# Block sums of weights for fourteen seven-product pairs: added in DRAM by transfers instead of on VectorE

## The chip, the cores and the metric

The kernel runs on one core of one Trainium2 chip. The metric is the device time of one execution in microseconds (us); the kernel before takes 1660.25 us, the median of 3 runs (1660.11 to 1660.39). Engines are named as in the profile: PE is TensorE's matmuls, PEld its weight loads, DVE is VectorE, ACT ScalarE, POOL GpSimd and SP SyncE. SP and Pool issue transfers here and compute nothing.

## The reference, cut to what matters

One block of a transformer on 256 positions of width 2048 in float32, with 256 positions of context beside it: a modulation of the inputs made from a condition vector, a gated recurrence in two directions with 8 heads, windowed attention with 8 heads, a gated merge of the two, and a feed-forward part with 5632 inner columns.

```python
mod = silu(cond) @ w_ada + b_ada                      # 6 vectors of 2048
px = modulate(x, norm1_g, mod[0], mod[1]) @ w_in       # the same for ctx
rec_x = recurrence(px...); att_x = windowed_attention(px...)
mix_x = gated_merge(rec_x, att_x, px[8], px[9], w_rec_proj, w_att_proj, w_out)
x_mid = x + mod[2] * mix_x
a, u = split(modulate(x_mid, norm2_g, mod[3], mod[4]) @ w_up)
ffn_x = (silu(depthwise_conv(a) ) * u) @ w_down
out = x_mid + mod[5] * ffn_x
```

The last four vectors of `mod` are needed late. The change concerns the product with `w_down` and, by where its transfers stand, the making of these vectors.

## The kernel before

All weights of the products lie in DRAM in one stream, `wst`, cut into halves of 128 x 1024 numbers (512 KB) in the order of their use. For each half SP issues a load into `raw` (five buffers), ACT rounds it to `whi`, DVE subtracts for the rest `wlo` (three buffers each), and PE multiplies with both: three matmuls stand for one product of full precision (`mm3`, L75). `Stream.load` (from L113) does this for most stages; `chunk` (from L144) for those where four blocks of 512 columns are combined.

The kernel runs the stages one after the other: the first projections, the modulation's first two vectors among them; the recurrence's gates and heads (`hgrn_a` to `hgrn_e`, tile `hb`); the attention (`att_scores`, `att_trans`, `att_out`); the gates and merge; `w_out`; the up products; the joint down stage (`down_two`); the last up and down products. Small work of the recurrence and the attention is kept in a list and put between the matmuls of the next products (`tick`).

The modulation's last four vectors are made beside all this. `ada_steps` (L476) is a generator of 128 steps. Each step loads a block of 512 KB into one of three or four `araw` buffers, by Pool's queue (L492), and DVE multiplies it by one column of the condition and adds it to `acc` (L495 for the first of 16 steps, L497 for the others). After 16 steps PE turns `acc` in two halves into PSUM (L505, pool `ms`, three banks, the same pool that the recurrence and the attention use) and DVE sums them into `modv`. `ada(n)` (L517) takes n steps at low priority; the stages call it at fixed places, and `Stream.load` by a pace.

In what order an engine gets its instructions is decided when the program is built: a scheduler places them by priority, by what they depend on and by its own notion of how long things take. On the chip each engine then works strictly in that order.

The joint down stage multiplies 16 pairs of blocks for each of two output halves. In seven of the 16 pairs (`SEVEN`) `half` (L175) uses seven products where eight would be needed; for that it wants, beside the blocks w21, w22 (load `rb`) and w11, w12 (load `ra`), four sums: t1 = w11 + w12, t3 = w12 + w22, t2 = t1 + w22, t4 = t2 + w21. DVE makes them by four additions of 128 x 512 (`four`, L228 to L231) into two `araw` buffers, and `chunk` rounds and splits these like loaded halves. The same function serves the gates' product (3 pairs in each of two halves) and the last down product.

Of the kernel before, what the change touches and what calls it, by code (L numbers as in the profile page):

```python
# [1 line left out]

# [5 lines left out]
F32 = mybir.dt.float32  # L8
# [3 lines left out]
ALU = mybir.AluOpType  # L12
AX = mybir.AxisListType

P = 128
T = 256
D = 2048
KT = D // P
# [16 lines left out]
FF_GROUPS = [(0, 16), (16, 16), (32, 12)]  # L35
SEVEN = (1, 3, 5, 7, 9, 11, 13)
# [18 lines left out]
def block_kernel(ctx, tc, xct, xr, prm, cst, ada2, wst, out):  # L55
    nc = tc.nc
# [9 lines left out]
    dram = ctx.enter_context(tc.tile_pool(name="dram", bufs=1, space=bass.MemoryType.DRAM))  # L66

    def bank(pool=None):
        pool = pool or mm
        return pool.tile([P, 512], F32, name="bank" + ("m" if pool is mm else "s"))  # L70
# [4 lines left out]
    def mm3(o, lh, ll, rh, rl, start, stop):  # L75
        mmul(o, lh, rh, start, False)
        mmul(o, lh, rl, False, False)
        return mmul(o, ll, rh, False, stop)
# [27 lines left out]
    class Stream:  # L106
# [26 lines left out]
        def next(self, n=1):  # L133
            if self.pos == 8:
                self.load()
            sl = slice(self.pos * P, (self.pos + n) * P)
            self.pos += n
            return self.hi[:, sl], self.lo[:, sl]

    st = Stream()  # L140
# [3 lines left out]
    def chunk(parts, make, tag="raw", home=None):  # L144
        with tc.high_priority(offset=min(LEAD, max(0, tc.tile_snap_priority() - base[0]))), ExitStack() as inorder:
            raw = strm.tile([P, 1024], F32, name=tag, bufs=5 if tag == "raw" else 2) if isinstance(tag, str) else tag
            hi, lo = home or [strm.tile([P, 1024], F32R, name=nm, bufs=3) for nm in ("whi", "wlo")]
            for b in behind:
                inorder.enter_context(tc.issue_after(b.ins))
            make(raw)  # L150
            w = slice(0, 512 * parts)
            a = S.copy(hi[:, w], raw[:, w])  # L152
            b = V.tensor_tensor(lo[:, w], raw[:, w], hi[:, w].bitcast(F32), op=ALU.subtract)  # L153
            behind[:] = [a, b]
        return raw, [(hi[:, 512 * i:512 * i + 512], lo[:, 512 * i:512 * i + 512]) for i in range(parts)]

    def fetch(raw):
        nc.sync.dma_start(raw, wst[st.half])
        st.half += 1

    def split(hi, lo, src):
        S.copy(hi, src)
        V.tensor_tensor(lo, src, hi.bitcast(F32), op=ALU.subtract)

    def combine(sev, y, post):
        S.copy(y[0], sev[0])
        V.tensor_tensor(y[2], sev[2], y[0], op=ALU.subtract)
        V.tensor_tensor(y[1], sev[1], y[2], op=ALU.add)
        V.tensor_tensor(y[2], sev[3], y[2], op=ALU.add)
        V.tensor_tensor(y[3], sev[3], y[1], op=ALU.add)  # L170
        if post:
            for b in range(4):
                post(b)

    def half(act, order, seven, sums, banks, y, own, made={}, post=None, tail=False):  # L175

        norm, sev = banks

        def add(b, a, w, start=False, stop=False):
            mm3(b, *a, *w, start, stop)  # L180
        seven = [p for p in order if p in seven]
        plains = [p for p in order if p not in seven]
        for p in order:
            k1, k2 = 2 * p, 2 * p + 1
            rb, (w21, w22) = chunk(2, fetch)
            a11, a21, a12, a22 = act(k1, 0), act(k1, 1), act(k2, 0), act(k2, 1)
            st0, plain = p == order[0], p == plains[0]
            if p not in seven:
                if p == order[-1]:
                    ra, (w11, w12) = chunk(2, fetch)  # L190
                    for b, u1, u2, v1, v2 in ((0, a11, a12, w11, w21), (1, a11, a12, w12, w22), (2, a21, a22, w11, w21),
                                              (3, a21, a22, w12, w22)):
                        for w in [slice(0, 512)] if not tail or b < 3 else [slice(0, 256), slice(256, 512)]:
                            add(norm[b][:, w], u1, [v[:, w] for v in v1])
                            add(norm[b][:, w], u2, [v[:, w] for v in v2], stop=True)
                    break
                add(norm[0], a12, w21, st0)
                add(norm[2], a22, w21, st0)
                add(norm[1], a12, w22, st0)
                add(norm[3], a22, w22, plain)  # L200
                ra, (w11, w12) = chunk(2, fetch)
                add(norm[0], a11, w11)
                add(norm[2], a21, w11)
                add(norm[1], a11, w12)
                add(norm[3], a21, w12)
                continue
            f, l = p == seven[0], p == seven[-1]
            if f:
                sev = sev()
            s1, s2, s4, *s3 = sums[p]  # L210
            add(norm[0], a12, w21, st0)
            add(norm[1], s4, w22, st0)
            ra, (w11,) = chunk(1, fetch, home=own)
            add(sev[0], a11, w11, f, l)
            if p in made:
                t1, t3, t2, t4 = made[p]
                add(sev[1], s1, t1, f, l)
                add(sev[3], s3[0] if s3 else a21, t3, f, l)
                add(sev[2], s2, t2, f, l)
                add(norm[2], a22, t4, st0)  # L220
                if l:
                    combine(sev, y, post)
                continue

            r4 = strm.tile([P, 1024], F32, name="araw", bufs=2)

            def four(raw):
                V.tensor_tensor(raw[:, 0:512], ra[:, 0:512], ra[:, 512:], op=ALU.add)  # L228
                V.tensor_tensor(raw[:, 512:], ra[:, 512:], rb[:, 512:], op=ALU.add)  # L229
                V.tensor_tensor(r4[:, 0:512], raw[:, 0:512], rb[:, 512:], op=ALU.add)  # L230
                V.tensor_tensor(r4[:, 512:], r4[:, 0:512], rb[:, 0:512], op=ALU.add)  # L231
            r2, (t1, t3) = chunk(2, four, "araw")
            add(sev[1], s1, t1, f, l)
            add(sev[3], s3[0] if s3 else a21, t3, f, l)

            _, (t2, t4) = chunk(2, lambda raw: None, r4)
            add(sev[2], s2, t2, f, l)
            add(norm[2], a22, t4, st0)
            if l:
                combine(sev, y, post)  # L240
        if post:
            return
        with tc.high_priority(offset=RUSH):
            for b in range(4):
                V.tensor_tensor(y[b], norm[b], y[b], op=ALU.subtract if b == 2 else ALU.add)
# [271 lines left out]
    def ada(n=1):  # L517
        with tc.high_priority(offset=-LAG), tc.issue_after(st.last.ins):
            for _ in range(n):
                next(ada_it, None)  # L520

    tasks = []

# [46 lines left out]
    def q_heads(h0):  # L570
        for h in range(h0, h0 + 4, 2):
            for i, o in enumerate(duo((xx, xx))):
                fold(qo[:, 0, h + i, :], o)
            ada(2)
        for h in range(h0, h0 + 4, 2):
            tmp = scr.tile([P, 512], F32, name="t")
            q2 = qo[:, 0, h:h + 2, :].rearrange("p h t -> p (h t)")
            exp_silu(q2, q2, tmp)
# [386 lines left out]
    for c in range(4):  # L965
        st.pace = 0
        if c % 2 == 0:
            norm = [bank() for _ in range(4)]
            y = [scr.tile([P, 512], F32, name="t") for _ in range(3)] + [scr.tile([P, 512], F32, name="rs", bufs=1)]
# [245 lines left out]
    def make(p, home):  # L1215
        rb, ra = [strm.tile([P, 1024], F32, name="raw", bufs=5) for _ in range(2)]
        for i, r in enumerate((rb, ra)):
            nc.sync.dma_start(r, wst[wst.shape[0] - 12 + 2 * LAST_ORDER.index(p) + i])
        r2, r4 = [strm.tile([P, 1024], F32, name="araw", bufs=2) for _ in range(2)]
        V.tensor_tensor(r2[:, 0:512], ra[:, 0:512], ra[:, 512:], op=ALU.add)  # L1220
        V.tensor_tensor(r2[:, 512:], ra[:, 512:], rb[:, 512:], op=ALU.add)
        V.tensor_tensor(r4[:, 0:512], r2[:, 0:512], rb[:, 512:], op=ALU.add)
        V.tensor_tensor(r4[:, 512:], r4[:, 0:512], rb[:, 0:512], op=ALU.add)
        for i, r in enumerate((r2, r4)):
            split(home[:, i, 0], home[:, i, 1], r)
        made[p] = [(home[:, i, 0, c:c + 512], home[:, i, 1, c:c + 512]) for i in range(2) for c in (0, 512)]
# [158 lines left out]
```

## Time and profile before

| what | us |
|---|---|
| median of 3 runs | 1660.25 |
| the profiled execution | 1660.26 |
| its span, first to last instruction | 1658.5 |
| PE busy | 1639.9 |
| DVE busy | 1303.1 |
| ACT busy | 861.8 |
| Pool busy | 68.7 |
| joint down stage, about | 1290 to 1457 |

The span is what the views of the profile divide up; 1.8 us of the execution lie around it. In the views, a group of instructions is a line, an engine, an operation and tiles, written out<-in with the count; then its busy time, the mean of one in ns, and the idle time before them with what ended it. A window is written as from:to, length, and then the busy time of PE, PEld, DVE, ACT and Pool, each with the number of instructions, the granted clock, the share of the DMA engines and GB/s. A wait is written as who, for whom, us in total, times and the longest.

### The profile page before, as it was taken

What the parts mean: (1) busy time and instruction counts of PE and PEld (TensorE: products, weight loads), DVE (VectorE), ACT (ScalarE), POOL (GpSimd) and SP (SyncE); (2) the same over time, 40 slices, a digit from 0 to 9 for tenths busy, and PEclk for the clock granted to TensorE, in tenths of its full rate; (3) what the DMA queues carried; (4) which work ended last, traced back from release to release, by engine and by line L of the source; (5) the groups of instructions that cost most, each with busy time, mean ns of one, the idle gap of its engine ahead of it and who ended that gap; (6) DMA issues with size and microseconds to landing.
All of it is one profiled execution on the core that took longest, in us unless ns stands there. A gap on an engine that the chain in (4) does not pass through costs nothing.

```text
span 1658.5 us, 23677 instructions
## 1 busy us (share of the span) xinstructions
PE 1639.9 (99%) x8827; PEld 1356.1 (82%) x8827; DVE 1303.1 (79%) x2001; ACT 861.8 (52%) x1302; POOL 68.7 (4%) x133
## 2 busy tenths in 40 slices
PE   7999999999999999999999999999999999999998
PEld 3668888888888888888888988888888888888887
DVE  3448986676889976888787798878877898998788
ACT  4336553443645664545445665555555555556552
POOL 0000100000000000000011000000000000000000
PEclk9999999999999999999999999999999999999999
DMA  9996834534455665676878467767655665666654
GB/s 380 408 373 241 300 115 153 204 114 150 167 205 202 222 215 176 233 284 213 310 262 307 175 238 263 251 226 267 235 193 185 203 207 199 222 207 222 220 186 162
DMA packets 104260, 377.03 MB, mean 227 GB/s; under 512 B 11696, under 2 KB 12112, under 8 KB 103888
## 3 DMA queue, kind: packets, MB, share of 16 engines
q1 hardware_dynamic: 85568, 307.87, 52.1%
q0 software_dynamic: 18576, 67.64, 12.4%
q8 instruction: 69, 1.13, 0.3%
q14 instruction: 47, 0.39, 0.1%
HBM read 373.36 MB, written 2.11 MB: 226 GB/s over the span
## 4 chain that ended last, share of the span: by engine, by line
PE 88%; DVE 4%; DMA 4%; issue 3%; ACT 1%; SPq 0%; POOL 0%; DVEq 0%; ACTq 0%; POOLq 0%
PE bankm L73 77%; PE banks L73 9%; DMA ringv<-in_wst_dram 1%; DMA ringq<-in_wst_dram 1%; DVE wlo L119 1%; DVE acc L497 1%; DMA ringkT<-in_wst_dram 1%; PE banks L505 0%; PE banks L872 0%; DMA araw<-in_ada_dram 0%; DMA xraw<-in_xct_dram 0%; ACT whi L118 0%; PE banks L697 0%; PE banks L705 0%; PE banks L900 0%
## 5 line engine op out<-in xcount | busy, mean ns | idle before, releaser
L73 PE MATMUL bankm<-hl,whi 128*128 128x512 f32 (+1 forms) x2048 | 626.6, 388 | 0.1
L118 ACT CAST whi<-raw 128x1024 fp32r<-128x1024 f32 (+1 forms) x378 | 394.5, 1045 | 393.2 <-PE bankm L73 338.9
L119 DVE TENSOR_TENSOR wlo<-raw,whi 128x1024 fp32r<-128x1024 f32 (+1 forms) x378 | 458.9, 1215 | 176.7 <-ACT whi L118 175.6
L73 PE MATMUL bankm<-whi,hl 128*128 128x512 f32 x1538 | 496.1, 393 | 1.3 <-ACT hl L340 0.9
L73 PE MATMUL bankm<-hl,wlo 128*128 128x256 f32 (+2 forms) x1760 | 396.1, 293 | 1.3 <-DVE wlo L119 1.3
L73 PEld LDWEIGHTS bankm<-hl,wlo 128*128 128x128 f32 x1760 | 330.5, 188 | 75.8 <-DVE wlo L119 2.1
L73 PEld LDWEIGHTS bankm<-hl,whi 128*128 128x128 f32 x2048 | 327.5, 189 | 17.7 <-DVE fs L1066 0.4
L73 PEld LDWEIGHTS bankm<-whi,hl 128*128 128x128 f32 x1538 | 288.0, 188 | 63.8 <-ACT hl L340 2.6
L73 PE MATMUL bankm<-wlo,hl 128*128 128x512 f32 x769 | 300.1, 391 | 0.0
L73 PEld LDWEIGHTS bankm<-wlo,hl 128*128 128x128 f32 x769 | 144.4, 188 | 28.9 <-DVE wlo L119 0.2
L497 DVE SCALAR_TENSOR_TENSOR acc<-araw,csil,acc 128x1024 f32<-128x1024 f32 x120 | 153.2, 1277 | 0.5
L153 DVE TENSOR_TENSOR wlo<-raw,whi 128x1024 fp32r<-128x1024 f32 x95 | 115.7, 1223 | 31.6 <-ACT whi L152 28.1
L152 ACT CAST whi<-raw 128x1024 fp32r<-128x1024 f32 x95 | 99.8, 1054 | 71.1 <-PE bankm L73 45.8
L492 POOL DMA_DIRECT2D araw<-in_ada_dram x128 | 67.9, 531 | 1111.9 <-DVE acc L497 635.5
L73 PE MATMUL bankm<-whi,yb 128*128 128x512 f32 x256 | 82.1, 396 | 0.0
L152 ACT CAST whi<-araw 128x1024 fp32r<-128x1024 f32 x44 | 46.2, 1053 | 62.4 <-DVE araw L229 56.2
L73 PEld LDWEIGHTS bankm<-whi,yb 128*128 128x128 f32 x256 | 47.9, 188 | 10.0
L153 DVE TENSOR_TENSOR wlo<-araw,whi 128x1024 fp32r<-128x1024 f32 x44 | 53.6, 1221 | 1.8 <-ACT whi L152 0.5
L73 PE MATMUL bankm<-wlo,yb 128*128 128x512 f32 x128 | 50.4, 394 | 0.0
L1079 ACT ACTIVATE fs<-fs,prm 128x256 f32<-128x256 f32 x44 | 26.4, 600 | 45.7 <-DVE fs L554 45.7
L73 PE MATMUL bankm<-whi,g 128*128 128x512 f32 x124 | 41.3, 389 | 0.0
L321 DVE TENSOR_REDUCE tn<-banks 128x8 f32<-128x32 f32 (+1 forms) x9 | 1.7, 187 | 46.1 <-ACT whi L118 42.9
(344 smaller groups left out, 1708.0 us busy)
## 6 DMA issues: line engine op xcount, KB each, us to landing
raw<-in_wst_dram SPq DMA_DIRECT2D x495, 512.0 KB, 4.0
araw<-in_ada_dram POOLq DMA_DIRECT2D x128, 512.0 KB, 4.6
ringv<-in_wst_dram SPq DMA_DIRECT2D x24, 512.0 KB, 9.9
ringq<-in_wst_dram SPq DMA_DIRECT2D x20, 512.0 KB, 9.9
araw<-in_wst_dram SPq DMA_DIRECT2D x10, 512.0 KB, 9.9
xraw<-in_xct_dram SPq DMA_DIRECT2D x8, 512.0 KB, 8.0
raw<-in_wst_dram SPq DMA_DIRECT2D x7, 384.0 KB, 9.9
ringkT<-in_wst_dram SPq DMA_DIRECT2D x5, 512.0 KB, 9.9
```

What stands on the lines that cost most here:

```text
L73: return PE.matmul(o, l, r, start=start, stop=stop, skip_group_check=True)
L118: S.copy(hi, raw)
L119: self.last = V.tensor_tensor(lo, raw, hi.bitcast(F32), op=ALU.subtract)
L152: a = S.copy(hi[:, w], raw[:, w])
L153: b = V.tensor_tensor(lo[:, w], raw[:, w], hi[:, w].bitcast(F32), op=ALU.subtract)
L321: V.tensor_reduce(m8, aps[:, 0:w].rearrange("p (q g c) -> p q c g", q=2 * n, g=4)[:, :, 0:2, :], axis=AX.X, op=ALU.add)
L492: nc.gpsimd.dma_start(raw, ada2[idx])
L497: V.scalar_tensor_tensor(acc, raw, csil[:, kt, 0:1], acc, op0=ALU.mult, op1=ALU.add)
L1079: S.activation(t, s, AF.Identity, bias=cb[:, f:f + 1], scale=cw[:, f, 1:2])
```

## The change

The fourteen seven-product pairs of the joint down stage (seven in each output half) get their four sums from DRAM. For each pair a block `sum` of 2 x 128 x 1024 numbers (1 MB) is laid out in DRAM. A copy fills it with `rb` and `ra` (L177 of the changed kernel), two transfers that add make t1 and t3 in its second part from `wst` (L179, L180), one makes t2 in the first part from t1 (L182) and one t4 from t2 (L184). All are issued by Pool's queue, four pairs at a time, one transfer per call of `ada`: 14 copies of 1 MB and 56 adding transfers of 256 KB, 70 in all. In the joint stage `half` then loads of `ra` only w11 (256 KB), and the two parts of the sum (512 KB each) by SP into the two `araw` buffers in which DVE built them before. DVE's four additions go; rounding, splitting and the matmuls stay. The other seven-product pairs are unchanged.

```diff
+    def fetch_half(raw):
+        nc.sync.dma_start(raw[:, 0:512], wst[st.half, :, 0:512])
+        st.half += 1
...
+    def sum_steps(group):
+        ds = []
+        for n, p in group:
+            at = JOINT + 32 * n
+            d = dram.tile([2, P, 1024], F32, name="sum%d" % len(dsums))
+            dsums[at, p] = d
+            ds.append((d, at + 2 * p))
+        for d, r in ds:
+            yield lambda: nc.gpsimd.dma_start(d, wst[r:r + 2])
+        for d, r in ds:
+            yield lambda: nc.gpsimd.dma_start(d[1, :, 0:512], wst[r + 1, :, 512:], accum_op=ALU.add)
+            yield lambda: nc.gpsimd.dma_start(d[1, :, 512:], wst[r, :, 512:], accum_op=ALU.add)
+        for d, r in ds:
+            yield lambda: nc.gpsimd.dma_start(d[0, :, 512:], d[1, :, 0:512], accum_op=ALU.add)
+        for d, r in ds:
+            yield lambda: nc.gpsimd.dma_start(d[0, :, 0:512], d[0, :, 512:], accum_op=ALU.add)
+
+    sum_all = [(n, p) for n in range(2) for p in SEVEN]
+    sum_it = (f for i in range(0, len(sum_all), 4) for f in sum_steps(sum_all[i:i + 4]))
...
-            ra, (w11,) = chunk(1, fetch, home=own)
+            ra, (w11,) = chunk(1, fetch_half if (at, p) in dsums else fetch, home=own)
...
+            if (at, p) in dsums:
+                d = dsums[at, p]
+                _, (t1, t3) = chunk(2, lambda raw: nc.sync.dma_start(raw, d[1]), "araw")
...
+                _, (t4, t2) = chunk(2, lambda raw: nc.sync.dma_start(raw, d[0]), "araw")
...
         with tc.high_priority(offset=-LAG), tc.issue_after(st.last.ins):
             for _ in range(n):
                 next(ada_it, None)
+            for f in itertools.islice(sum_it, 1):
+                f()
```

The change also moves instructions that it does not name, since the whole order is built anew. Lines of the changed kernel stand 1 to 43 higher than those of before (L497 is L538, L505 is L546, L119 is L120). Three places show it.

Pool's queue, from the start of the program. Before, it holds the modulation's loads one behind the other (`gate` is a late row of the first of the four vectors):

```order
L1380 UNCONDITIONAL_BRANCH
L492 DMA araw<-in_ada_dram 128x1024 x83
L955 DMA gate_7178<-line 128x1024
L492 DMA araw<-in_ada_dram 128x1024 x45
L1380 UNCONDITIONAL_BRANCH
```

After, with `sum_1149` and the next names for the blocks in DRAM:

```order
L1423 UNCONDITIONAL_BRANCH
L177 DMA sum_1149<-in_wst_dram 16x16384
L533 DMA araw<-in_ada_dram 128x1024 x4
L177 DMA sum_1150<-in_wst_dram 16x16384
L533 DMA araw<-in_ada_dram 128x1024
L177 DMA sum_1151<-in_wst_dram 16x16384
L533 DMA araw<-in_ada_dram 128x1024
L177 DMA sum_1152<-in_wst_dram 16x16384
L533 DMA araw<-in_ada_dram 128x1024
L179 DMA sum_1149<-in_wst_dram 128x512
```

The first copy has moved to the head of the queue, where one modulation load stood, and the other transfers stand between the loads.

DVE's order in the recurrence. Before, around half 35 of the weights (halves are counted here by their `wlo`), the modulation's steps stand singly or a few together between halves and the recurrence's instructions (`hb`, `qo`):

```order
L645 TENSOR_TENSOR hb<-hb,qo 128x256
L497 SCALAR_TENSOR_TENSOR acc<-araw,csil,acc 128x1024
L119 TENSOR_TENSOR wlo<-raw,whi 128x1024
L649 TENSOR_TENSOR hb<-hb 128x512
L497 SCALAR_TENSOR_TENSOR acc<-araw,csil,acc 128x1024
L554 TENSOR_TENSOR qo<-bankm,qo 128x256 x2
L119 TENSOR_TENSOR wlo<-raw,whi 128x1024
L497 SCALAR_TENSOR_TENSOR acc<-araw,csil,acc 128x1024
L254 TENSOR_TENSOR qo<-qo,t 128x512
L497 SCALAR_TENSOR_TENSOR acc<-araw,csil,acc 128x1024
L119 TENSOR_TENSOR wlo<-raw,whi 128x1024
```

After, the 16 halves up to half 61 stand together, and behind them come the steps that belong before and after half 35 in the order above:

```order
L670 TENSOR_SCALAR hb<-hb,lb_t 128x512
L120 TENSOR_TENSOR wlo<-raw,whi 128x1024 x16
L538 SCALAR_TENSOR_TENSOR acc<-araw,csil,acc 128x1024 x12
L547 TENSOR_REDUCE modv<-banks 128x4 x2
L536 TENSOR_SCALAR acc<-araw,csil 128x1024
L549 TENSOR_TENSOR modv<-modv,prm 128x8
L733 COPY_PREDICATED hb<-cst,banks 128x256
L735 COPY_PREDICATED hb<-cst,banks 64x2x64
L538 SCALAR_TENSOR_TENSOR acc<-araw,csil,acc 128x1024
```

The steps of the modulation have moved behind some 26 later halves, and the recurrence's instructions of the same time with them; the next `wlo` stands 111 instructions behind half 61.

PE's order at the attention. Before, a few of its matmuls (`hl` with `ab` are scores) stand between those of weights (`whi`, `wlo` with `hl`):

```order
L73 MATMUL bankm<-whi,hl 128x512
L73 MATMUL banks<-hl,ab 128x512 x9
L73 MATMUL bankm<-whi,hl 128x512
L73 MATMUL bankm<-wlo,hl 128x512
L73 MATMUL bankm<-whi,hl 128x512 x2
L73 MATMUL bankm<-wlo,hl 128x512
```

After, three of the four groups of scores, turns (L915) and outputs (`ab` with `hl`) stand one behind the other:

```order
L74 MATMUL banks<-hl,ab 128x512 x3
L915 MATMUL banks<-cst,gr 128x128 x16
L74 MATMUL banks<-ab,hl 128x512 x12
L74 MATMUL banks<-hl,ab 128x512 x12
L915 MATMUL banks<-cst,gr 128x128 x16
L74 MATMUL banks<-ab,hl 128x512 x12
L74 MATMUL banks<-hl,ab 128x512 x12
L915 MATMUL banks<-cst,gr 128x128 x16
L74 MATMUL banks<-ab,hl 128x512 x12
```

The attention has moved behind the weights of the stages with which it was interleaved; between its parts PE now has nothing else in its order.

More of the change, by code (lines that the diff above doesn't have):

```diff
@@ L1 @@
+import itertools
 from contextlib import ExitStack
@@ L159, in fetch @@
         st.half += 1
+    def fetch_half(raw):
+        nc.sync.dma_start(raw[:, 0:512], wst[st.half, :, 0:512])
+        st.half += 1
+    dsums = {}
+    JOINT = wst.shape[0] - 24 - 2 * FF_GROUPS[2][1] * KT // 8 - 64
+    def sum_steps(group):
[16 more added lines that the diff above has]
+    sum_it = (f for i in range(0, len(sum_all), 4) for f in sum_steps(sum_all[i:i + 4]))
     def split(hi, lo, src):
@@ L177, in half @@
         norm, sev = banks
+        at = st.half
         def add(b, a, w, start=False, stop=False):
@@ L218, in half @@
                 add(sev[3], s3[0] if s3 else a21, t3, f, l)
+                add(sev[2], s2, t2, f, l)
+                add(norm[2], a22, t4, st0)
+                if l:
+                    combine(sev, y, post)
+                continue
+            if (at, p) in dsums:
+                d = dsums[at, p]
+                _, (t1, t3) = chunk(2, lambda raw: nc.sync.dma_start(raw, d[1]), "araw")
+                add(sev[1], s1, t1, f, l)
+                add(sev[3], s3[0] if s3 else a21, t3, f, l)
+                _, (t4, t2) = chunk(2, lambda raw: nc.sync.dma_start(raw, d[0]), "araw")
                 add(sev[2], s2, t2, f, l)
```

## The prediction

> **What bounds the kernel now.** I read the page's busy shares and chain first, then the windows of the stage that the change is made for, then the waits, and last the groups by form, for prices.
>
> ```profile
> span 1658.5 us, 23677 instructions
> PE 1639.9 (99%) x8827; PEld 1356.1 (82%) x8827; DVE 1303.1 (79%) x2001; ACT 861.8 (52%) x1302; POOL 68.7 (4%) x133
> ...
> PE 88%; DVE 4%; DMA 4%; issue 3%; ACT 1%; SPq 0%; POOL 0%; DVEq 0%; ACTq 0%; POOLq 0%
> ...
> 1290.00:1457.00 167.00, 166.74 (x736) 137.15 (x735) 149.97 (x174) 91.57 (x100) 0.00 (x0) 1.00 0.62 209
> ...
> 1350.00:1400.00 50.00, 50.00 (x222) 41.43 (x221) 44.42 (x51) 26.32 (x28) 0.00 (x0) 1.00 0.59 201
> ```
>
> PE is busy for 1639.9 of 1658.5 us and carries 88% of the chain. A busy PE need not be at its peak, so I look at its pace: 222 matmuls in 50 us, all of 512 columns here, are 0.225 us each, and in the joint down stage (1290 to 1457 us) PE stands still for 167.00 - 166.74 = 0.26 us. DVE is nearly as full there (149.97 us), but nobody on the chain waits for it. The profiled execution took 1660.26 us, 1.8 us of it around the span, and the median of the runs is 1660.25, so the sum is made on 1660.3.
>
> PE keeps this pace because DVE always has the next half of weights (its `wlo`) ready:
>
> ```profile
> POOL araw L492 <- DVE acc L497: 635.5, 95, 71.4
> ...
> DVE wlo L119 <- ACT whi L118: 175.6, 143, 4.7
> ...
> raw<-in_wst_dram SPq DMA_DIRECT2D x495, 512.0 KB, 4.0
> araw<-in_ada_dram POOLq DMA_DIRECT2D x128, 512.0 KB, 4.6
> ```
>
> `whi` and `wlo` have three buffers, so at most three halves lie ahead of PE. A half feeds 24 matmuls of 512 columns (5.4 us) or, where two banks are filled, 12 (2.7 us). The reserve is thus 16 or 8 us; anything longer that stands between two `wlo` on DVE stops PE. The modulation's loads are slowed only by their own steps on DVE (Pool waits 635.5 us for those to free a buffer).
>
> **The change, part by part.** *The joint stage.* Gone are four additions for each of 14 pairs:
>
> ```profile
> L228 DVE TENSOR_TENSOR araw<-raw 128x512 f32<-128x512 f32 x14 | 9.6, 683 | 0.0
> ```
>
> With L229 to L231 alike, that is 4 x 9.6 = 38 us of DVE. It buys at most PE's 0.26 us there; I book nothing. That the sums come too late is excluded: Pool's last adding transfer stands before the 79th of the modulation's 128 loads. What replaces it: per pair 0.25 MB less of `ra` and 1 MB of sums more, 11 MB over 167 us, or 209 + 66 = 275 GB/s. The trace has carried more beside a full PE:
>
> ```profile
> 850.00:900.00 50.00, 50.00 (x232) 41.33 (x231) 45.79 (x46) 27.24 (x40) 7.91 (x15) 1.00 0.93 342
> ...
> raw<-in_wst_dram SPq DMA_DIRECT2D x7, 384.0 KB, 9.9
> ```
>
> The new wait is SP's, for one of the two `araw` buffers; behind it queue the next `raw` loads, and PE waits for those last. A buffer comes round once per plain and seven-product pair, 24 + 21 matmuls or 10.1 us; a load of 4.0 us fits, the slowest, 9.9 us plus 2 us of ACT and DVE, misses by about 2, so the bounds are 0 and 14 x 2 = 28 us. The stage's own pace is nearest the 4.0 row: 0.
>
> *The start.* Pool's first transfer, which waits for nothing, was one modulation load and is now a copy of 1 MB within DRAM.
>
> ```profile
> 1.25 0.66 POOL L492 DMA_DIRECT2D araw<-in_ada_dram  x1 [0.81 <-POOLq L1373]
> ...
> 50.00:100.00 50.00, 50.00 (x291) 32.33 (x290) 21.98 (x49) 16.80 (x27) 0.00 (x0) 1.00 1.03 407
> ```
>
> The DMA engines are full, 407 GB/s here, while the first stage runs. The copy replaces 0.5 MB: 0.5 MB more at 407 GB/s is 1.3 us; counted as read and written, 1.5 MB is 3.9. I take 2.5 us.
>
> *The order, which is the large part.* The 70 transfers stand between the modulation's loads on Pool, and the order in which the program was built has its steps on DVE elsewhere. Before, the steps lie singly or in small groups between `wlo`. Now they stand in lumps (the pieces of the order above): after half 61 the next `wlo` comes behind 111 other instructions, 21 of them modulation steps; after half 75 behind 54 (8 steps); after 77 behind 25 (5); after 141 behind 136 (14 steps and the whole attention softmax); after 143 behind 37 (16); after 223 behind 16 and then 9 more (16 in the two). PE's order has the modulation's transposes, the recurrence and the attention at the same places, and each engine works in its order, so PE cannot go round them and the next `wlo` cannot overtake on DVE. The prices:
>
> ```profile
> L497 DVE SCALAR_TENSOR_TENSOR acc<-araw,csil,acc 128x1024 f32<-128x1024 f32 x120 | 153.2, 1277 | 0.5
> ...
> L119 DVE TENSOR_TENSOR wlo<-raw,whi 128x1024 fp32r<-128x1024 f32 x369 | 450.0, 1221 | 174.4 <-ACT whi L118 173.3
> L118 ACT CAST whi<-raw 128x1024 fp32r<-128x1024 f32 x369 | 386.9, 1050 | 390.6 <-PE bankm L73 338.9 <-issue 36.5 <-PE banks L73 5.4
> ...
> 0.00:1658.00 1658.00, 40.18 (x752) 35.91 (x752) 112.56 (x323) 78.25 (x184) 1.00 0.65 227
> ```
>
> The last row is the recurrence's tile `hb` alone: 112.56 us for 323 instructions of DVE, 0.348 each. A lump begins when PE has freed the buffer of its last `wlo`: 1.05 us of ACT and 1.22 of DVE, 2.3 us, come first.
>
> - After 61: 21 steps (26.3 us), 87 of the recurrence (30.3), three small ones and the `wlo` (2.7), 2.3: 61.6 us. PE has halves 59 to 61 (72 matmuls, 16.2 us) and some 5 us of small ones: it stands 40 us. Halves 63 and 64 then have 20 and 23 recurrence instructions ahead, 8.2 and 9.2 us against 5.4: 7 us.
> - After 75: 9.7 + 43 x 0.348 + 2.7 + 2.3 = 29.7 us, against 54 matmuls and 2 us of small ones, 14.2: 16 us. After 77: 6.4 us of steps, some 7 of key work, 2.4 for two `wlo`, against 30 matmuls: 9 us.
> - After 141 and 143:
>
> ```profile
> L861 DVE TENSOR_REDUCE tn<-banks 128x1 f32<-128x512 f32 x16 | 11.0, 686 | 0.1
> L867 DVE TENSOR_SCALAR gr<-gr,tn 128x512 f32<-128x512 f32 x16 | 7.7, 481 | 0.1
> L859 DVE TENSOR_TENSOR banks<-banks,cst 128x128 f32<-128x128 f32 x16 | 4.7, 294 | 3.9 <-PE banks L73 3.7
> L862 DVE TENSOR_SCALAR tn<-tn,nsink 128x1 f32<-128x1 f32 x16 | 3.3, 207 | 0.1
> L866 DVE RECIPROCAL tn<-tn 128x1 f32<-128x1 f32 x16 | 2.5, 155 | 0.0
> L865 DVE TENSOR_TENSOR tn<-tn 128x1 f32<-128x1 f32 x16 | 2.4, 153 | 0.1
> L163 DVE TENSOR_TENSOR ab<-banks,ab 128x512 fp32r<-128x512 f32 x20 | 13.1, 682 | 2.7 <-ACT ab L162 2.7
> ```
>
> The first six rows are 31.6 us, 17 of the last kind at 0.682 are 11.6, and four more of that form (L883) 2.8: 46 us. With 14 steps (17.3), 3.0 of small ones and `wlo`, and 2.3 the first lump is 69 us. The second has 19.9 us of steps, 16 other instructions of 128x512 or 128x128, some 9 us at 0.68 and less, and 4 of small ones and two `wlo`: 33. Against both PE has 96 matmuls of scores and outputs (21.6 us), 64 transposes (5) and halves 139 to 143 in part (57 matmuls, 12.8): it stands 102 - 39 = 63 us.
> - After 223: 15 x 1.277 + 0.75 + 8 of others and two `wlo` + 2.3 = 30 us, against 65 matmuls and some turns, 16 us: 14 us.
>
> Sum with DVE never pausing: 40 + 7 + 16 + 9 + 63 + 14 = 149 us. But it must pause.
>
> ```profile
> 150.94 0.53 POOL L492 DMA_DIRECT2D araw<-in_ada_dram  x1 [6.48 <-DVE acc L495]
> ...
> L162 ACT CAST ab<-banks 128x512 fp32r<-128x512 f32 x20 | 11.1, 589 | 2.8 <-PE banks L845 1.7 <-PE banks L872 1.1
> ```
>
> Of the long rows of steps some 32 come after the buffers that were filled ahead; four buffers turn in 1.28 + 0.53 + 4.6 us, 1.6 us a step, three in 2.1, so 10 to 27 us more, say 17. In the lumps the softmax and the recurrence meet ACT and PE in turn; by the idle time behind rows such as L859's (3.7 us) and ACT's copy of 0.59 us it is 2 to 5 us for each of four groups and 2 us a head: 12 to 30, say 18. About 60 of the 70 transfers stand among these loads, each with Pool's 0.53 us: 0 to 32, say 10. So 45 us more, between 22 and 89.
>
> *Relief.* The steps leave the stretch from 150 to 212 us, where DVE was full and PE did stand:
>
> ```profile
> 150.00:212.00 62.00, 60.48 (x445) 51.31 (x443) 61.10 (x110) 37.86 (x67) 8.43 (x16) 1.00 0.80 278
> ```
>
> That gives back at most 62.00 - 60.48 = 1.5 us. Sum: 1660.3 + 149 + 45 + 2.5 - 1.5 = **1855 us**.
>
> **The rivals.** *The lumps are hidden.* If DVE did its lumps while PE had other work, what is left is 1.3 to 3.9 at the start, 0 to 1.5 back, and the joint stage's 0.26: 1660 to 1664 us, no slower than a measurement can tell. For it speaks that DVE is idle for 355 us in all and that the same work fits today. It decides if no lump is longer than PE's reserve: 16 us against 62 and 69 speaks against it. 6 in 100.
>
> *Slow restarts.* PE's first matmuls after its longest wait today took longer than later ones of the same form:
>
> ```profile
> 8.08 5.39 PE L73 MATMUL bankm<-t,cst 128*128 128x512 f32 x8 [8.08 <-ACT t L355]
> ...
> 17.82 1.88 PE L73 MATMUL bankm<-t,cst 128*128 128x512 f32 x4
> ```
>
> 0.67 against 0.47 us each: 8 x 0.2 = 1.6 us for a restart; with some 25 standstills (six lumps, in each about four places where PE turns to a tile that DVE has still to make) 40 us, so 1895. Against it: the granted clock is 1.00 in every window, and those first ones also waited for their inputs. The Trainium skill ("TensorE: Matmul & The Clock Gate", Part 1) says that an idle window of about 3.4 us puts the array at half its clock until it has been busy as long; by that I estimate 1.7 us a restart and 43 in all. The trace has no long standstill that could show it. 20 in 100.
>
> *Slow transfers.* A copy or an adding transfer within DRAM is not in the trace. The nearest rows:
>
> ```profile
> out_dram<-xn SPq DMA_DIRECT2D x3, 256.0 KB, 2.1
> ...
> ringv<-in_wst_dram SPq DMA_DIRECT2D x24, 512.0 KB, 9.9
> ```
>
> At 2.1 us they disappear between two loads. If instead some 30 that stand inside the long rows each hold the next load for a further landing of 4.6 us, it is 140 us more, near 1995. The adding ones read what they write and must wait for the one before, which speaks for the slower end; the free engines while PE stands speak for the faster. The Trainium skill ("DMA: Bandwidth & Descriptors", Anatomy of one DMA) gives 2.0 us and bytes at 436 GB/s, an estimate of 2.6 us for 256 KB, nearer the faster end; it would leave the sum as it is. 12 in 100.
>
> **How the numbers follow.** My forecast alone has 62 in 100, the slow restart 20, slow transfers 12, hidden lumps 6 (5 of them within 0.2%, 1 faster, if the relief outweighs the start by more than I find). About 0.2%, 3.3 us, is what a measurement of this kernel can tell from no change. The range goes down to 149 less a seventh, for reserve that I did not count, with no pause at all, since steps could fill them: 1660 + 128, about 1790. It goes up to 149 + 89 of pauses, 28 in the joint stage and 3.9 at the start: 1660 + 270 = 1930, which takes in the slow restart. Beyond it lie the slow transfers and the hidden lumps, 18 in 100. Slower 94, same 5, faster 1.
>
> **What would show it.** After: PE's busy share falls to about 88%, with a few dark slices where the modulation runs and none in the joint stage; PE waits for DVE `acc`, `hb` and the attention's tiles, tens of us in all; the chain moves from PE to DVE. Right in the detail: the joint stage still takes 167 us, with DVE near 112. Wrong if PE stands in the joint stage, if the slices in the middle stay full, or if the acc steps wait for their loads longer than they run.

## The result: 1899.9 us, slower by 14.5%

| | before | after |
|---|---|---|
| median of 4 runs, us | 1660.32 | 1899.87 (1896.62 to 1903.14) |
| the profiled execution | 1660.26 | 1903.14 |
| its span | 1658.5 | 1901.4 |
| PE busy | 1639.9 | 1707.0 |
| PE standing | 18.6 | 194.4 |

The ratio is 1.1447, with an interval of 1.1433 to 1.1461. The forecast was 1855 in a range of 1790 to 1930. From the page of the changed kernel, the busy shares, PE and its granted clock in 40 slices, and the chain:

```profile
span 1901.4 us, 23805 instructions
PE 1707.0 (90%) x8827; PEld 1389.9 (73%) x8827; DVE 1279.3 (67%) x1945; ACT 866.9 (46%) x1303; POOL 125.9 (7%) x203
...
PE   7999999488599993738999569999999999999998
...
PEclk9999999699799996768999779999999999999999
...
PE 78%; DVE 6%; DMA 6%; issue 6%; ACT 2%; POOL 1%; SPq 0%; DVEq 0%; POOLq 0%; ACTq 0%
```

The dark slices lie where the order of the changed kernel has its lumps, and in nearly the same slices the granted clock is at 6 to 8 tenths (digits 6 to 8) instead of 9 or more. There are two losses, not one: PE stands 194.4 - 18.6 = 175.8 us longer, and the same 8827 matmuls keep it busy for 1707.0 - 1639.9 = 67.1 us longer. Together they are the span's 242.9 us. The windows of the four places, then the joint stage and the stretch of the relief (length, PE, PEld, DVE, ACT, Pool, granted clock, DMA share, GB/s):

```profile
325.00:400.00 75.00, 41.34 (x321) 32.77 (x321) 52.48 (x97) 19.48 (x47) 25.20 (x37) 0.76 0.82 235
475.00:525.00 50.00, 28.40 (x173) 22.30 (x174) 36.65 (x73) 15.74 (x39) 10.55 (x18) 0.75 0.56 205
700.00:875.00 175.00, 97.71 (x346) 70.60 (x345) 105.83 (x190) 53.41 (x101) 45.62 (x66) 0.70 0.68 207
1050.00:1125.00 75.00, 39.64 (x134) 28.25 (x134) 35.49 (x35) 14.28 (x21) 15.48 (x25) 0.73 0.61 191
...
1533.00:1700.00 167.00, 167.00 (x740) 137.91 (x740) 117.36 (x118) 92.22 (x101) 0.00 (x0) 1.00 0.82 271
...
150.00:212.00 62.00, 62.00 (x458) 53.28 (x457) 49.25 (x97) 38.39 (x66) 4.10 (x7) 1.00 0.71 257
```

PE stands 33.7, 21.6, 77.3 and 35.4 us in the four, 167.9 of the 194.4. In the joint stage, the only one whose work was changed, it does not stand at all. What PE waits for in the four places, and what the modulation's steps and Pool wait for, from the waits (us, times, longest):

```profile
PE banks L546 <- DVE acc L538: 109.1, 5, 26.1
DVE acc L538 <- DMA araw<-in_ada_dram: 42.1, 31, 3.0
POOL sum L184 <- DMA sum<-sum: 11.7, 5, 3.9
```

The transposes of `acc` (L546) stand in PE's order in front of its next work, and five times PE waits up to 26 us for the last step of a lump. DVE's steps themselves wait 42.1 us for loads.

### The profile page after: what moved, and what is told of

It reads as the page before. It is cut to its first block, busy times and chain, and to the rows that moved or that the text cites. A ratio compares the mean times of both kernels' runs of the same rounds, so it can differ in the third digit from the quotient of the medians.

```text
span 1901.4 us, 23805 instructions
## 1 busy us (share of the span) xinstructions
PE 1707.0 (90%) x8827; PEld 1389.9 (73%) x8827; DVE 1279.3 (67%) x1945; ACT 866.9 (46%) x1303; POOL 125.9 (7%) x203
## 3 DMA queue, kind: packets, MB, share of 16 engines
q8 instruction: 69, 1.13, 0.2%
## 4 chain that ended last, share of the span: by engine, by line
PE 78%; DVE 6%; DMA 6%; issue 6%; ACT 2%; POOL 1%; SPq 0%; DVEq 0%; POOLq 0%; ACTq 0%
PE bankm L74 67%; PE banks L74 9%; DMA araw<-in_ada_dram 3%; DVE acc L538 2%; DMA sum<-sum 1%; DVE wlo L120 1%; DMA raw<-in_wst_dram 1%; ACT whi L119 1%; PE banks L915 1%; DMA ringv<-in_wst_dram 1%; DMA ringq<-in_wst_dram 1%; POOL araw L533 0%; DMA xraw<-in_xct_dram 0%; DVE tn L904 0%; PE banks L546 0%
## 5 line engine op out<-in xcount | busy, mean ns | idle before, releaser
L120 DVE TENSOR_TENSOR wlo<-raw,whi 128x1024 fp32r<-128x1024 f32 (+1 forms) x378 | 459.3, 1217 | 329.8 <-ACT whi L119 329.4
L119 ACT CAST whi<-raw 128x1024 fp32r<-128x1024 f32 (+1 forms) x378 | 394.7, 1045 | 474.4 <-PE bankm L74 439.5
L538 DVE SCALAR_TENSOR_TENSOR acc<-araw,csil,acc 128x1024 f32<-128x1024 f32 x120 | 153.6, 1280 | 43.0 <-DMA araw<-in_ada_dram 42.1
L533 POOL DMA_DIRECT2D araw<-in_ada_dram x128 | 76.7, 599 | 1283.5 <-DVE acc L538 1008.4
L546 PE MATMUL banks<-cst,acc 128*128 128x128 f32 x64 | 16.5, 370 | 109.1 <-DVE acc L538 109.1
L74 PE MATMUL bankm<-whi,yb 128*128 128x512 f32 x256 | 88.3, 420 | 6.8 <-ACT whi L119 6.8
L546 PEld LDWEIGHTS banks<-cst,acc 128*128 128x128 f32 x64 | 11.1, 191 | 112.3 <-issue 77.6
L74 PE MATMUL bankm<-wlo,yb 128*128 128x512 f32 x128 | 55.0, 430 | 4.8 <-DVE wlo L120 4.8
```

The costliest lines, as they stand in the source:

```text
L74: return PE.matmul(o, l, r, start=start, stop=stop, skip_group_check=True)
L119: S.copy(hi, raw)
L120: self.last = V.tensor_tensor(lo, raw, hi.bitcast(F32), op=ALU.subtract)
L533: nc.gpsimd.dma_start(raw, ada2[idx])
L538: V.scalar_tensor_tensor(acc, raw, csil[:, kt, 0:1], acc, op0=ALU.mult, op1=ALU.add)
L546: PE.transpose(ps[:, n * P:(n + 1) * P], acc[:, (4 * hf + n) * P:(4 * hf + n + 1) * P], ident)
```

## The experiments

The theory was that the new order costs the time: lumps on DVE make PE stand, and its standing slows its clock. The rivals were the transfers themselves (Pool's queue, DMA engines), and the joint stage's new loads. Each ratio is to the kernel before as run beside that run, with its interval in brackets.

### The same transfers in an order without lumps

Each copy is cut in two, and Pool is held to the order in which the program names its transfers. The order then has no lump.

```diff
+    onpool = []
+    def pool_dma(*args, **kw):
+        with ExitStack() as inorder:
+            for b in onpool:
+                inorder.enter_context(tc.issue_after(b.ins))
+            onpool[:] = [nc.gpsimd.dma_start(*args, **kw)]
...
-            yield lambda: nc.gpsimd.dma_start(d, wst[r:r + 2])
+            yield lambda: pool_dma(d[0], wst[r])
+            yield lambda: pool_dma(d[1], wst[r + 1])
```

The adding transfers and the modulation's loads go through `pool_dma` too.

> The same sums are made by the same bytes between the modulation's loads, but each copy of 1 MB goes as two of 512 KB, and Pool keeps the order in which the program names its transfers. In the order built from this no gap between two wlo of DVE is longer than 10 us (by the durations of the trace of before), where the changed kernel has seven, 223 us in all. If the order is the cause (the lumps and the slow clock that they bring), this takes 1660 to 1668 us: 2 us for the start, and a few for steps that wait for a load. If the transfers are the cause (they hold Pool's queue and the DMA engines, so the steps' loads land late), it stays near the changed kernel, 1800 to 1900, with DVE's acc steps waiting for araw for far more than 42 us. If the joint stage were the cause, it would stay at 1900.

It took 1666.43 us, 1.004 of before (1.0028 to 1.0053). From its page:

```profile
span 1664.6 us, 23780 instructions
PE 1642.8 (99%) x8827; PEld 1356.1 (81%) x8827; DVE 1270.4 (76%) x1945; ACT 861.9 (52%) x1302; POOL 133.6 (8%) x217
...
PEclk9999999999999999999999999999999999999999
```

The same 28 MB are written for the sums and the sums are read, PE is full and its clock is whole. In its trace no two neighbouring `wlo` behind the first 130 us end more than 10 us apart; in the changed kernel the two longest distances are 69 and 101 us. DVE's steps wait 10.2 us for loads instead of 42.1. Of 240 us, some 233 are gone with the lumps. The same traffic in another order costs 6 us.

### Pool's order kept, the copies whole

The same `pool_dma`, but the copy of 1 MB in one piece; the order has six lumps.

> Copies of 1 MB as in the changed kernel, only Pool keeps the order in which the program names its transfers, as in the run with two copies of 512 KB. The order built from it has six long gaps, 234 us. If the order is the cause, 1890 to 1920 us, by its gaps 11 us above the changed kernel; so that the gain of the run with two copies does not come from Pool's order. If the transfers are the cause, the same as with two copies of 512 KB, within 20 us.

1902.87 us, ratio 1.1448 (1.1424 to 1.1471), as the order theory had it. So holding Pool's order is not what helped; the cut of the copies is. That it helps by the order that is built from it, and not because one copy of 1 MB is worse for the DMA engines than two of 512 KB, no run shows by itself, since none has whole copies and an order without lumps. The waits speak for the order: in the changed kernel DVE's steps wait 42.1 us for loads in all, while PE stands 175.8 us longer, and in the run with idle instructions on DVE, further down, PE stands by lumps alone.

### The joint stage alone, and the sums alone

In one run the sums are not made, and the joint stage's two loads come from the weights:

```diff
+    dsums = {(JOINT + 32 * n, p): wst[JOINT + 32 * n + 2 * p:JOINT + 32 * n + 2 * p + 2] for n in range(2) for p in SEVEN}
...
-            for f in itertools.islice(sum_it, 1):
-                f()
```

> No sums are made. The joint stage loads the two parts of 512 KB per pair from the weights' own rows in DRAM, so its results are not the reference's there; its transfers, roundings and matmuls are those of the changed kernel, and DVE's additions are gone. No gap between two wlo is longer than 10 us. If the order is the cause, 1660 us, within 2, and the joint stage takes 167 us at about 275 GB/s with DVE near 112 us in it. If the joint stage's new loads cost something, up to 28 us more, 1688, and PE stands there.

1659.12 us, ratio 0.9993 (0.9985 to 1.0002): no difference that can be told. In the other run the sums are made and not read (`if (at, p) in dsums` becomes `if False`, and `fetch_half` becomes `fetch`):

> The sums are made in DRAM as in the changed kernel, but not read: the joint stage adds on DVE as before. The order has the changed kernel's seven long gaps, 223 us. By the order and by the transfers alike, 1895 to 1903 us, since the joint stage gives and takes nothing; if the joint stage's loads cost something, less by that.

1900.12 us, ratio 1.1446 (1.1431 to 1.1462). The joint stage neither gives nor takes; the loss comes with the making of the sums. The first start of PE in the two (start, us, then the wait in brackets), joint stage alone first:

```profile
8.10 7.47 PE L74 MATMUL bankm<-t,cst 128*128 128x512 f32 x10 [8.10 <-ACT t L377]
```

```profile
10.28 7.58 PE L74 MATMUL bankm<-t,cst 128*128 128x512 f32 x10 [10.28 <-ACT t L396]
```

With a modulation load at the head of Pool's queue PE starts at 8.1 us, as before; with the copy of 1 MB there, at 10.3. That is the start's price, 2.2 us.

### Lumps without any transfer

To see what a lump alone does to PE, the kernel before got idle instructions on DVE ahead of the `wlo` of five halves (16, 24, 40, 72 and 32 of them), in the up stages, where PE is otherwise full:

```diff
+            for _ in range(STALLS.get(wst.shape[0] - self.half, 0)):
+                with tc.high_priority(offset=LEAD + 1), tc.issue_after((stall or self.last).ins):
+                    stall = V.tensor_tensor(idle, cst_t[:, 0:512], cst_t[:, 0:512], op=ALU.max)
...
+                    if stall:
+                        behind_it.enter_context(tc.issue_after(stall.ins))
```

> The kernel before, with no sums in DRAM. At five halves of the two up stages DVE gets 16, 24, 40, 72 and 32 idle instructions of 128x512 (about 0.68 us each, 125 us in all), behind which the half's wlo stands; in the order built from it the five gaps between two wlo are 14, 22, 34, 55 and 30 us. If a lump on DVE alone makes PE stand, PE stands there for each gap less about 5 us (its reserve of three halves of 2.75 us each, less the 3.5 us of a first rounding and wlo): 9 + 17 + 29 + 50 + 25 = 130 us. On top comes what a standstill costs afterwards: if the granted clock falls only for a fixed time behind each standstill, 1.7 to 3 us each, 9 to 15 in all, so 1800 us; if it falls in proportion to the time stood (67 of 176 us in the changed kernel, 0.38), 50 us, so 1840. If the changed kernel's slow clock came from its transfers, the clock stays at 1.00 here and the time is 1790.

1797.49 us, ratio 1.0832 (1.0817 to 1.0847). PE's busy time, and its wait for the five `wlo` (two short waits are in the row as well):

```profile
PE 1652.9 (92%) x8827; PEld 1365.7 (76%) x8827; DVE 1424.9 (79%) x2185; ACT 862.3 (48%) x1302; POOL 68.7 (4%) x133
...
PE bankm L74 <- DVE wlo L131: 124.3, 7, 48.9
```

PE stood 8.6, 15.2, 28.5, 48.9 and 21.8 us, where 9, 17, 29, 50 and 25 were expected: gap less reserve comes within 3.2 us each time. And without any transfer in DRAM its busy time grew by 1652.9 - 1639.9 = 13.0 us, 2.6 for each standstill on the mean. Windows of 2 us around the longest show how (the clock is the third number from the end):

```profile
1314.00:1316.00 2.00, 0.26 (x2) 0.00 (x0) 2.00 (x6) 0.30 (x1) 0.00 (x0) 1.00 0.02 4
1316.00:1318.00 2.00, 0.00 (x0) 0.00 (x0) 2.00 (x6) 0.51 (x1) 0.00 (x0) 0.73 0.00 0
1318.00:1320.00 2.00, 0.00 (x0) 0.00 (x0) 1.97 (x4) 0.00 (x0) 0.00 (x0) 0.50 0.00 0
...
1362.00:1364.00 2.00, 0.87 (x3) 0.87 (x4) 2.00 (x2) 0.00 (x0) 0.00 (x0) 0.50 0.48 133
1364.00:1366.00 2.00, 2.00 (x7) 1.61 (x7) 1.35 (x2) 0.00 (x0) 0.00 (x0) 0.50 0.73 154
1366.00:1368.00 2.00, 2.00 (x9) 1.71 (x8) 0.00 (x0) 0.62 (x1) 0.00 (x0) 0.50 0.93 358
1368.00:1370.00 2.00, 2.00 (x13) 1.77 (x12) 1.23 (x1) 0.43 (x1) 0.00 (x0) 0.97 0.96 385
```

PE's last matmul ends at 1314.3; the clock falls to 0.50 in the window from 1316 to 1318. PE starts again at 1363.1, and for 5 us, up to just behind 1368, it works at half its pace: 7 to 9 matmuls in 2 us, then 13. At half pace, 5 us of work lose 2.5. The windows from PE's restart to the return of the clock, for the standstills of 28.5 and 21.8 us:

```profile
1225.60:1231.60 6.00, 6.00 (x19) 5.23 (x20) 2.89 (x3) 1.04 (x1) 0.00 (x0) 0.50 0.72 200
1654.90:1658.20 3.30, 3.30 (x11) 2.91 (x12) 2.18 (x2) 0.00 (x0) 0.00 (x0) 0.50 0.74 179
```

In the order of time the five ways back took 3.9, 4.8, 6.0, 5.0 and 3.3 us, behind standstills of 8.6, 15.2, 28.5, 48.9 and 21.8 us: they do not follow the length. Half of their 23 us is 11.5 of the 13.0. The Trainium skill ("TensorE: Matmul & The Clock Gate", Part 1) gives about 3.4 us for the idle window and for the way back, with a phase that varies; the trace agrees on the half clock, and has 3.3 to 6.0 us for the way back.

### The same lumps, PE kept busy

Behind PE's last matmul ahead of each standstill stands a row of matmuls on constants, whose results are not used:

```diff
+            if stall:
+                b = bank(ms)
+                with tc.issue_after(lastmm[0].ins):
+                    for _ in range(WARM[wst.shape[0] - self.half]):
+                        mmul(b[:, 0:P], ident, ident, True, True)
```

> The same five gaps on DVE, but behind PE's last matmul ahead of each stands a row of 34, 72, 148, 300 and 110 matmuls of 128x128 on constants (0.128 us each at full speed, 85 us in all), whose results are not used. If PE's standing lowers the granted clock, the clock stays at or near 1.00 and the time is that of the run without the row less the slow part, 10 to 50 us below it: about 1790. If the slow clock has another cause, the time and the clock are the same as without the row, or longer by what of the 85 us the gaps don't hide.

1810.92 us, ratio 1.0912 (1.0897 to 1.0927). PE and its clock, and the filling row's own group:

```profile
PE 1788.4 (99%) x10155; PEld 1505.7 (83%) x10155; DVE 1425.1 (79%) x2185; ACT 862.8 (48%) x1302; POOL 68.7 (4%) x133
...
PEclk9999999999999999999999999999999999999999
...
L75 PE MATMUL banks<-cst 128*128 128x128 f32 x1328 | 149.1, 275 | 0.0
```

The time did not fall as expected: each of the 664 matmuls stands in the records twice, and the row took 149.1 us instead of the 85 that I had reckoned, 26 more than PE stood (123.0). But the clock answers the question. The work itself took 1788.4 - 149.1 = 1639.3 us, as in the kernel before (1639.9), against 1652.9 where PE stood. It is the standing that slows the clock.

### Copies only

The adding transfers are left out; the joint stage reads the bare copies. The order has three lumps.

> Only the 14 copies of 1 MB are made, none of the 56 adding transfers; the joint stage reads the copies, so its sums are left out and its results are not the reference's. The order has three gaps over 10 us: 50.5, 63.5 and 11 us. If the order is the cause, PE stands about 50.5 + 4 - 21 = 33, 63.5 + 4 - 18 = 50 and 5 us, 88 in all, and at the changed kernel's ratio of lost time to standing (243 to 176) 120 us are lost: 1770 to 1790 us, with the standing in two places. If each transfer costs its share, 14 of 70, it is 48 us: 1708.

1748.34 us, ratio 1.0536 (1.0521 to 1.0550): outside both forecasts, 22 us under the one by the order and 40 over the one by the transfers' number. PE's busy time and its long waits:

```profile
PE 1657.7 (95%) x8827; PEld 1367.2 (78%) x8827; DVE 1272.2 (73%) x1945; ACT 863.2 (49%) x1302; POOL 75.6 (4%) x147
...
PE banks L539 <- DVE acc L531: 52.7, 2, 28.0
```

PE stands 1745.8 - 1657.7 = 88.1 us of the span, 69.5 more than before, where 88 more were expected, in two places as the order had it: the two long waits are 24.7 and 28.0 us, where I had 33 and 50. Its busy time grew by 17.8, a quarter of the standing and not the 0.38 that I had put on top. The clock falls to 0.50 six times here: at the two long standstills and at four of 2.0 to 3.7 us. PE works 24.3 us in these stretches, so the slow clock makes 12 of the 17.8; the rest is open.

### What is left of the transfers: 6 us

The run with the same transfers was 6 us above before. Four runs look for them. The sums not read (as in "the sums alone", but in the order without lumps):

> Like the run with the same transfers, but the sums are not read: the joint stage adds on DVE as in the kernel before. If the 6 us come from the making of the sums, 1665 to 1668 us. If the joint stage's new loads make them, 1660 to 1661.

1667.66 us, ratio 1.005 (1.0038 to 1.0063): the 6 us come from the making of the sums. With two transfers per call (`itertools.islice(sum_it, 2)`):

> Like the run with the same transfers and Pool's forced order, but two transfers per call, so the last stands before the 54th of the modulation's loads instead of the 90th and none is left in the stretch from 844 to 871 us, where in that run the last adding transfers held Pool's queue and DVE's acc steps waited 9.7 us. If that stretch made most of its 6 us, this takes 1659 to 1662 us and PE has 50.0 us of work in 850 to 900. If the crowding only moves, it stays at 1664 to 1670 with the waits elsewhere.

1670.78 us, ratio 1.007 (1.0056 to 1.0083), just above the second range. Windows of the run with one transfer per call:

```profile
150.00:200.00 50.00, 49.16 (x333) 42.16 (x333) 49.87 (x82) 31.38 (x56) 14.05 (x24) 1.00 0.99 383
200.00:250.00 50.00, 49.31 (x363) 41.09 (x362) 42.72 (x102) 24.52 (x49) 6.63 (x10) 1.00 0.61 182
...
850.00:900.00 50.00, 45.16 (x198) 34.44 (x197) 40.94 (x41) 22.33 (x34) 10.68 (x19) 1.00 1.01 345
```

And of this one:

```profile
150.00:200.00 50.00, 46.08 (x315) 38.92 (x314) 44.91 (x75) 28.80 (x52) 16.67 (x25) 1.00 1.03 369
200.00:250.00 50.00, 42.94 (x321) 35.52 (x320) 36.54 (x85) 22.62 (x44) 9.68 (x15) 0.93 0.76 244
850.00:900.00 50.00, 50.00 (x234) 41.16 (x233) 46.72 (x49) 24.29 (x33) 8.81 (x17) 1.00 0.93 346
```

The loss at 850 to 900 us went, and a larger one came at 150 to 250, where the transfers now crowd. Most of the loss in 200 to 250 is one wait of 7.1 us that begins at 213, behind a step that waited 3.8 us for its load. The DMA engines are full where the losses arise: 1.01 in 850 to 900 of the first run, 1.03 in 150 to 200 and 1.08 from 200 to 213 us in the second. But Pool also waits 51 us for sums in the second run, so the two causes are not yet apart. Seven pairs at a time, so that no adding transfer waits long for the one before (`sum_steps` over groups of 7):

> Like the run with the same transfers (two copies of 512 KB, Pool's forced order, one transfer per call), but seven pairs at a time instead of four, so an adding transfer stands seven behind the one whose result it needs, in the last group too (there it was two). If what is left of that run's 6 us is Pool held by adding transfers that wait for each other (14.7 us there, 11.9 of it in 850 to 871 us), ahead of loads that DVE's acc steps then wait for, this takes 1659 to 1663 us, with PE full in 850 to 900. If it is the traffic itself (28 transfers of 512 KB and 56 of 256 KB on full DMA engines), it stays at 1665 to 1668.

1665.13 us, ratio 1.0034 (1.0021 to 1.0048). A miss for the waits: Pool now waits 2.3 us for sums instead of 14.7, and PE still loses 5.2 us in 850 to 900, where a step waits 6.6 us for a load that was issued among adding transfers. What is left is the traffic: loads that land late beside the transfers, whether for the full DMA engines (share 1.00) or for their place in Pool's queue. So the last run puts all transfers where there is room:

```diff
+            turn[0] += n
-            for f in itertools.islice(sum_it, 1):
+            for f in itertools.islice(sum_it, 2 if turn[0] > 22 else 0):
```

> Like the run with seven pairs at a time, but the first transfer stands behind the 20th of the modulation's loads and two go per call, so that the last stands behind the 64th: all of them fall where the DMA engines of before are busy for 0.40 to 0.63 of the time (250 to 700 us), none in 150 to 200 (0.82) and 850 to 900 us (0.93). No gap between two wlo is longer than 10 us. If what the transfers cost once the order is kept is their traffic on full DMA engines, 1658 to 1661 us, with PE full in 850 to 900 and 49.7 of 50 in 200 to 250. If the transfers cost something wherever they stand, 1664 to 1668.

1659.91 us, ratio 1.0003 (0.9994 to 1.0012). Its page, three windows, and the landing times of its transfers:

```profile
PE 1640.6 (99%) x8827; PEld 1356.4 (82%) x8827; DVE 1270.3 (77%) x1945; ACT 862.6 (52%) x1302; POOL 132.5 (8%) x217
...
450.00:500.00 50.00, 46.88 (x276) 36.93 (x275) 38.52 (x73) 21.87 (x37) 8.83 (x18) 1.00 0.99 366
550.00:600.00 50.00, 49.94 (x235) 40.95 (x234) 43.03 (x74) 31.14 (x50) 18.02 (x23) 1.00 1.07 315
850.00:900.00 50.00, 50.00 (x234) 41.34 (x233) 46.94 (x47) 27.01 (x39) 7.91 (x15) 1.00 0.98 370
...
sum<-in_wst_dram POOLq DMA_DIRECT2D x28, 512.0 KB, 12.9
sum<-in_wst_dram POOLq DMA_DIRECT2D x28, 256.0 KB, 12.1
sum<-sum POOLq DMA_DIRECT2D x28, 256.0 KB, 10.6
```

The whole change, sums made and read, costs nothing that can be told here, though its copies of 512 KB land more slowly than in any other run (12.9 us against 7.8 to 8.9). Two things partly cancel: PE starts at 6.9 us instead of 8.1, as in the other runs that hold Pool's order, and in 450 to 500 us it stands 2.6 us longer than before. There the transfers have filled the DMA engines (0.99; 0.63 before); in 550 to 600 us they are as full (1.07) and PE loses nothing. So a full stretch can cost, and need not. Nor does the change gain: DVE's 33 us were never on the path, and no version beat the kernel before.

## Why the prediction was right in kind and short in size

**The joint stage, booked at 0.** Right. The roundings of the stage's `raw` halves (shortest, median and longest, then first and last start), before and after:

```profile
L152 ACT CAST whi<-raw x50: 1042/1056/1060, 1285.3 to 1448.7; 128x1024 fp32r<-128x1024 f32 x50
```

```profile
L153 ACT CAST whi<-raw x50: 1048/1056/1056, 1528.9 to 1691.5; 128x1024 fp32r<-128x1024 f32 x50
```

163.4 us became 162.6. The traffic was 271 GB/s for a forecast of 275. DVE fell from 149.97 to 117.36 us, not to 112: the 56 additions are gone, 38.2 us by their own durations, but instructions that stand close behind one another overlap in the records, so only 32.6 us of busy time went.

**The start, 2.5 us.** Measured 2.0 (PE's first matmul at 10.07 instead of 8.08); without any copy it was 8.10, and 6.9 in the runs that hold Pool's order.

**The relief, 1.5 us.** Right: PE is now busy for all of 150 to 212 us.

**The lumps, 149 us, and the pauses, 45.** Shown as the cause by the run without lumps and by the run with lumps alone. Together they came to about 175 of the forecast 194. By place, without pauses, I had 47, 25, 63 and 14 us and the trace, pauses included, has 33.7, 21.6, 77.3 and 35.4. The last was the worst: ten steps in a row took 22.9 us (1082.7 to 1105.6), 2.3 us a step and not the 1.28 of the bare instruction, since six of them waited 9.9 us for their loads while five adding transfers stood between these, and PE had already waited six times 1.13 us ahead of it. The steps' waits for loads were 42.1 us in all, where I had 17 + 10 for buffers and Pool. The first was shorter than its instructions; why was not tried.

**The clock, the step that failed.** The sum took the pace of PE's matmuls as that of before and left their slowing to a rival at 20 in 100. PE was busy 67.1 us longer, more than that rival's 40. In windows of 0.5 us the granted clock of the changed kernel goes down to 0.50 twenty times within the span. PE works 100.7 us in these stretches, so at half pace the slow clock makes 50 of the 67, 2.5 for each, where the rival had 25 times 1.6. The other 17 lie at a clock of 1.00, and no run shows what made them. That twenty is near the rival's 25 is in part luck: in the 7 us ahead of ten of the twenty PE had not stood longer than 1.7 us at a time, and the rival did not count such waits. The longest stretch of it is the attention, where PE turns every few us to a tile that is not there, and the clock falls anew for each head. Two windows of 4 us from it, and one behind a wait of 1.13 us ahead of the last lump:

```profile
754.00:758.00 4.00, 3.03 (x11) 2.34 (x11) 2.45 (x4) 2.15 (x4) 0.00 (x0) 0.50 0.96 401
770.00:774.00 4.00, 2.97 (x11) 2.28 (x10) 2.57 (x4) 2.15 (x4) 0.00 (x0) 0.50 0.00 0
1063.50:1066.90 3.40, 3.40 (x9) 2.62 (x10) 0.00 (x0) 0.00 (x0) 0.00 (x0) 0.50 0.45 154
```

I had argued that the clock was 1.00 in every window before. That was no evidence: behind its start the kernel before had no standstill longer than 0.9 us.

**The slow transfers, 140 us.** The transfers were slow, 7.7 to 9.8 us to land where I had hoped for 2.1, but the price of it was small: 6 us for the same transfers in an order without lumps. In the lumps they are a part of the 42.1 us.

**The chain.** I expected it to move from PE to DVE; it has PE at 78% and DVE at 6%. The waits showed the cause; the chain did not.

Lumps and pauses came out 19 us under the forecast and the clock 67 over it: 48 too low in the sum (by the profiled execution; 45 by the median), inside the range.

## What to carry to other kernels

Where a build sets the order, a transfer's shape can change it: look first at what now stands between the instructions that feed the full engine, and price each gap as its length less the engine's reserve, plus some 2.5 us of slow clock for each time that the granted clock falls. Work taken from an engine that nobody waited for gained nothing here, though it was 33 us. Background transfers cost least where the DMA engines had room; place them by the share in the windows, not by how fast they land, and look which load then lands late.

## What the runs showed of the hardware

- What a standstill costs afterwards does not follow its length: behind standstills of 9 to 49 us PE worked 3.3 to 6.0 us at a clock of 0.50. For each fall of the clock PE worked 4.6 us at half pace there (mean of five), 4.0 with the copies alone (six) and 5.0 in the changed kernel (twenty), which is 2.0 to 2.5 us lost.
- Waits of 1.13 us that come again and again went with four falls of the clock between 1050 and 1081 us of the changed kernel, each 3.4 us long. Such waits do not always: in the run with two transfers per call PE waited 1.5 and 1.3 us at 175 and 182 us, and the clock stayed at 1.00. What decides it is not shown.
- Copies and adding transfers within DRAM, from the view of the changed kernel's transfers (KB each, median us to landing; the last row is the copies of 1 MB):

```profile
araw<-in_ada_dram POOLq DMA_DIRECT2D x128, 512.0 KB, 6.1
...
sum<-in_wst_dram POOLq DMA_DIRECT2D x28, 256.0 KB, 8.4
sum<-sum POOLq DMA_DIRECT2D x28, 256.0 KB, 7.7
...
sum<-in_wst_dram POOLq DMA_DIRECT2D x14, 9.8
```

An adding transfer of 256 KB lands later than a load of 512 KB, both beside other traffic. The Trainium skill ("DMA: Bandwidth & Descriptors", Anatomy of one DMA) gives the 2.0 us and the 436 GB/s by which I had estimated 2.6 us; the trace does not agree, with 7.7 and 8.4. No run has such a transfer alone.
